# Context keys and values in float32 parts, first expert weights in idle buffers, token low parts on GpSimd: a mixture-of-experts kernel on one core

## The chip, the core and the metric

The kernel is one program on one core of a Trainium2 chip. The core has a matrix engine (PE), a vector engine (DVE), an activation engine (ACT), GpSimd (POOL), and SyncE (SP), which here does nothing but issue DMA transfers from DRAM. The metric is the time of one execution on the device in microseconds; lower is better.

## What is computed

The reference is a first block (a hybrid mixer, cross attention to a memory, a mixture of 32 experts) and a second block (a hyena branch, differential attention over the tokens and over a context, a feed-forward part), for 256 tokens of width 1024 in float32. The parts that matter here:

```python
# mixture of experts: top group, then top 2 of its 8 experts
hb = jax.nn.silu(xb @ w1[e]) * (xb @ w3[e])      # w1, w3: 1024 x 512
return hb @ w2[e]                                # w2: 512 x 1024
...
return rmsnorm(x, norm_f_g)                      # end of the first block
...
# second block: keys and values of the context, 256 rows
hc = modulate(rmsnorm_2(ctx, g_mix_pre[layer]), csh1, csc1)
kv_c = hc @ w_in[layer][:, OFF_K:OFF_G]          # 512 columns of keys, 512 of values
...
k_all = jnp.concatenate([k, k_c], axis=1)
v_all = jnp.concatenate([v, v_c], axis=1)
```

The context keys and values depend on nothing in the first block, and nothing reads them before the attention of the second block.

## The kernel before

**Weights.** Every weight goes through a ring of 1 MB buffers ("slots") in the order of the code. `wtile` takes the next slot, and the load into it, issued by SP, waits for the product that read the slot last. SP issues in order, so one load that waits holds back all loads behind it. `change_ring` adds or removes slots: during the expert stage there are 16, and from pair 6 on, when `filters` gives ten of them to other uses, 8.

**Two kinds of product.** `dense` and `dense_T` take a float32 product apart into three faster ones: `split` makes a high part of each weight block (`wh`, ACT, L303) and a low part (`wl`, DVE, L304), and PE multiplies high by high, high by low, low by high (L315 to L317, L351 to L353). The expert stage multiplies float32 directly (L1274, L1304).

**Order of the work around the change.** After the cross attention (`wxo`) the tokens are transposed and multiplied by the router's weights (`lg`). DVE then works out the routing: which token goes to which slot of which expert, as matrices `hot` (L938). In the same stretch ACT and DVE make high and low parts of the normed tokens, `xnh` (L868) and `xnl` (L869), with a stride of 8 elements. PE gathers tokens by products of `xnh` and `xnl` with `hot` (`pxg`, L944), ACT copies them to `xg` (L945), and the first expert product can start. PE's waiting times in routing are filled with the context products: `ctx_k` (keys) and `ctx_v` (values), both three-part, both ahead of the first expert product.

**The expert stage** runs over 16 pairs of experts, j = 0 to 15. For each, `up` takes w1 (`hw1`, four loads of 1 MB) and w3 (`hw3`, four loads), and `down` of the pair before takes w2 (four loads): 192 MB in all. A half of `up` is two loads and is named `kb` 0 or 1 below. Between them stand the scatter of results (`py`), the gather for the next pairs (`pxg`) and, from pair 7 on, pieces of the hyena filters (`f` to `fH`).

**After the last pair** the first block's last norm runs on ACT, DVE and POOL, and its result `xs` is transposed (L273) and split for the second block's first products.

A list scheduler orders the instructions of each engine; `issue_after` and `pe_after` place an instruction behind another one on its engine.

Of the kernel before, what the change touches and what calls it, by code (L numbers as in the profile page):

```python
# [8 lines left out]
F32 = mybir.dt.float32  # L9
# [8 lines left out]
P = 128  # L18
D = 1024
S = 256  # L20
# [81 lines left out]
def _body(nc, tc, I, out, ctx, dbg):  # L102
# [28 lines left out]
    def f(t):  # L131
        return t.bitcast(F32)
# [32 lines left out]
    def wloads(wsrc, c0, n, KB=8):  # L165
        return [wload(wsrc[kb * P:(kb + min(4, KB - kb)) * P, c0:c0 + n], min(4, KB - kb), n) for kb in range(0, KB, 4)]
# [109 lines left out]
    def tr_split(src, KB, gcol=None, sc=1.0, bcol=None, hl=None, name="t", g="A"):  # L276

        hi, lo = hl if hl else (xTt(name + "h", g), xTt(name + "l", g))
        for kk in range(0, KB, 2):
            pv = tr4(src, kk)  # L280
            if gcol is None:
                hilo(hi[:, kk:kk + 2, :], lo[:, kk:kk + 2, :], pv, sc)
                continue
            for j in range(2):
                k = kk + j
                if bcol is None:
                    hilo(hi[:, k, :], lo[:, k, :], pv[:, j, :], gcol[:, k:k + 1])
                else:
                    last["hi"] = A.activation(hi[:, k, :], pv[:, j, :], AF.Identity, bias=bcol[:, k:k + 1],  # L289
                                              scale=gcol[:, k:k + 1])  # L290
                    lo_of(lo[:, k, :], hi[:, k, :], pv[:, j, :], gcol[:, k:k + 1], bcol[:, k:k + 1])
        return hi, lo
# [43 lines left out]
    def dense_T(xh, xl, KB, ws, n, consume, ahead=None):  # L336


        nb = n // P
        accs = [acc().rearrange("p (b s) -> p b s", b=2) for _ in range(0, nb, 2)]  # L340
        for k in range(KB):
            if ahead:
                ahead(k)
            h, l = split(ws[k // 4][:, k % 4, :], n)
            if pend:
                pend.pop(0)()
            for b in range(nb):
                s = slice(b * P, (b + 1) * P)
                p = accs[b // 2][:, b % 2, :]

                T.matmul(p, h[:, s], xh[:, k, :], start=k == 0 and b % 2 == 0, stop=False)  # L351
                T.matmul(p, h[:, s], xl[:, k, :], start=False, stop=False)  # L352
                T.matmul(p, l[:, s], xh[:, k, :], start=False, stop=k == KB - 1 and b in (nb - 1, b // 2 * 2 + 1))  # L353
            if k % 4 == 3 and after:
                after.pop(0)()
        for i, p in enumerate(accs):
            consume(i, p[:, :min(2, nb - 2 * i), :])
# [42 lines left out]
    def copy_to(dst, **kw):  # L400
        def c(t, p):
            A.activation(dst[:, t, :], p, AF.Copy, **{k: v[:, t:t + 1] for k, v in kw.items()})
        return c
# [401 lines left out]
    softmax(0)  # L805
    softmax(1)
    wxo = [wloads(I["w_xo"][0], ch * 512, 512) for ch in range(2)]
    wck = [wloads(I["w_in_2"][0], 2048 + ch * 512, 512) for ch in range(2)]
    for ch in range(2, 4):
        dense(mh, ml_, 8, W["w_xkv", ch], 512, copy_to(vx[:, :, (ch - 2) * 512:(ch - 1) * 512], scale=rm))  # L810
    oh, ol = xTt("oh", "A"), xTt("ol", "A")
# [11 lines left out]
    rc = rsq(sumsq(cx), 2, 1.0 / D)  # L823
    for t in range(2):
        V.tensor_scalar(cx[:, t, :], cx[:, t, :], rc[:, t:t + 1], None, op0=OP.mult)
    ch_, cl_ = tr_split(cx, 8, mods[:, 1, :], bcol=mods[:, 6, :], name="cx", g="B")
    for ch in range(2):
        dense(oh, ol, 8, wxo[ch], 512, add_x(ch))
    tap("x2", x)
# [19 lines left out]
    xmT = xgt("xmT")  # L849
    for kk in range(0, 8, 2):  # L850
        pv = tr4(x, kk)
        A.activation(xmT[:, kk, :], pv[:, 0, :], AF.Copy, scale=g_moe[:, kk:kk + 1])
        V.tensor_scalar(xmT[:, kk + 1, :], pv[:, 1, :], g_moe[:, kk + 1:kk + 2], None, op0=OP.mult)
    rxm = rsq(sumsq(x), 2, 1.0 / D, name="rxm", pl=mo)
    p = smp("lg")
# [4 lines left out]
    def in_block(v, k):  # L860
        return v.rearrange("t (p k) -> t k p", k=k)

    def by_row(v, k):
        return v.rearrange("t (k p) -> t k p", k=k)

    xn = [xTt(nm, "A", F32R, (P, 2, D)) for nm in ("xnh", "xnl")]
    for t in range(2):
        A.activation(by_row(xn[0][:, t, :], 8), in_block(x[:, t, :], 8), AF.Copy, scale=rxm[:, t:t + 1])  # L868
        V.scalar_tensor_tensor(by_row(xn[1][:, t, :], 8), in_block(x[:, t, :], 8), rxm[:, t:t + 1],  # L869
                               by_row(f(xn[0][:, t, :]), 8), op0=OP.mult, op1=OP.subtract)  # L870
    lg = mo.tile([P, 2, 36], F32, name="lg")
    for t in range(2):
        V.scalar_tensor_tensor(lg[:, t, :], p[:, 36 * t:36 * t + 36], rxm[:, t:t + 1], brt, op0=OP.mult, op1=OP.add)
# [85 lines left out]
    V.tensor_copy(pre_, p[:, :96].rearrange("p (c n) -> p c n", c=3))  # L959


    def ctx_k():
        def c_kc(i_, p):
            A.activation(kTc[:, 2 * i_:2 * i_ + 2, :], p, AF.Copy)
        dense_T(ch_, cl_, 8, wck[0], 512, c_kc)

    def ctx_v():
        dense(ch_, cl_, 8, wck[1], 512, copy_to(vc))
        change_ring(["xTB"] * 2)
    ctx_k()  # L970
    ctx_v()


    ge = mo.tile([P, 2, 4], F32, name="ge")
# [157 lines left out]
    def filters():  # L1132
# [5 lines left out]
        wc = late["wc"] = ExitStack()  # L1138
        wpC = late["wpC"] = wc.enter_context(tc.tile_pool(name="wpC", bufs=2, side="right", reuse_waits="tile"))
        change_ring([wpC] * 2, (wpB,))  # L1140
        fctx = late["fctx"] = ExitStack()
        fp = fctx.enter_context(pool("fp", "right"))
        dft = fp.tile([P, 2, 2, S], F32, name="dft")
# [89 lines left out]
    def erows(nm, e, b0, n):  # L1233

        return I[nm][0, e].rearrange("(p k) n -> p k n", p=P)[:, b0:b0 + n, :]

    def eload(nm, e, kb, k, n):
        v = wtile(k, n)
        nc.sync.dma_start(v, erows(nm, e, kb * k, k))
        return v  # L1240

    def norm_part(t, hf, xs):

# [24 lines left out]
    def up(j, nm, hps, kbs):  # L1268
        s0 = (j % 2) * P
        for kb in kbs:  # L1270
            we = [eload(nm, 2 * j + e, kb, 4, 512) for e in range(2)]
            for k in range(4):
                for e in range(2):
                    traced[:] = [T.matmul(hps[64 * e:64 * e + 64, :], xgs[j][:, 4 * kb + k, s0 + 64 * e:s0 + 64 * e + 64], we[e][:, k, :],  # L1274
                                start=kb + k == 0, stop=kb + k == 4)]

    def act_half(hps):
# [12 lines left out]
    def down(j, hT):  # L1290
        po = [acc("po0"), acc("po1")]
        for kb in range(2):
            if j < NJ - 1:
                we = [eload("w2", 2 * j + e, kb, 2, 1024) for e in range(2)]
            else:

                we = [wtile(2, 1024) for e in range(2)]
                for q in range(2):
                    for e in range(2):
                        nc.sync.dma_start(we[e][:, q, :], erows("w2", 2 * j + e, 2 * kb + q, 1)[:, 0, :])  # L1300
            for q in range(2):
                for hf in range(2):
                    for e in range(2):
                        traced[:] = [T.matmul(po[hf][64 * e:64 * e + 64, :], hT[:, 2 * kb + q, 64 * e:64 * e + 64],  # L1304
                                    we[e][:, q, hf * 512:(hf + 1) * 512], start=kb + q == 0, stop=kb + q == 2)]
        return po

    def gather_some(n):
# [19 lines left out]
    for j in range(NJ):  # L1328
        if j == 2:
            with pe_after():  # L1330
                po = down(1, hT)
            with pe_after():
                gather_some(2)
            after_down(1, po)
            hT = None
            traced.clear()
            overflow(n_over)
            traced.clear()
        if j % 2 == 0 and j + 2 < NJ:
            xg_, st_ = group(j + 2)  # L1340
            xgs[j + 2] = xgs[j + 3] = xg_
            todo += st_
        h1 = acc("hw1")
        with pe_after():
            up(j, "w1", h1, (0, 1))
        sg = act_half(h1)
        if j in (6, 15):
            hooks[j]()
        po = None
        if hT is not None:  # L1350
            with pe_after():
                po = down(j - 1, hT)
        h3 = acc("hw3")
        with pe_after():
            up(j, "w3", h3, (0, 1))
        V.tensor_tensor(by_row(sg, 4), by_row(sg, 4), in_block(h3, 4), op=OP.mult)  # L1356
        if j == 0:
            lambdas()
            n_over = nc.values_load(novi[0:1, 0:1], min_val=0, max_val=7)
            with pe_after():  # L1360
                bc_rows(rows[:, 0], dest)
                bc_rows(rows[:, 1], gt)
        if po is not None:
            after_down(j - 1, po)
        with pe_after():
            gather_some(4)
        if 6 < j < 15 and j in hooks:
            with pe_after():
                hooks[j]()
        with pe_after():  # L1370
            hT = turn(sg)
    with pe_after():
        po = down(NJ - 1, hT)
    after_down(NJ - 1, po, norm_part)
    tap("x3", x)
    moctx.close()

# [18 lines left out]
    with tc.issue_after(last["hi"].ins):  # L1396
        for t in range(2):
            A.activation(x[:, t, :], xr[:, t, :], AF.Copy, scale=r1[:, t:t + 1])
    tap("xp", x)
    late["wc"].close()  # L1400
    set_ring([wpA] * NA)
# [294 lines left out]
```

## Time and profile before

| | |
|---|---|
| median of 3 runs | 1289.45 us (1285.69 to 1291.61) |
| the profiled execution: its own time, its span | 1290.93 us, 1289.1 us |
| PE, DVE, ACT, POOL busy in the span | 1234.1, 747.4, 552.7, 69.3 us |
| bytes moved | 365.29 MB, mean 283 GB/s |

The span goes from the first to the last instruction of the profiled execution. A busy time counts how long an engine had an instruction, not what that instruction could have taken at best. Positions ("at 388.22") are microseconds from the start of the span.

### The profile page before, as it was taken

To read this page: it belongs to the slowest core of one execution; us is meant where nothing else is said; L and a number is where in the kernel's file an instruction comes from. 1 tells how busy PE (TensorE), PEld (TensorE's weight loads), DVE (VectorE), ACT (ScalarE), POOL (GpSimd) and SP (SyncE) were. 2 spreads that over 40 slices of the span, in tenths; PEclk is the share of its full clock that TensorE was granted. 3 is DMA by queue.
4 is the path that set the end of the run, shared out by engine and by line. 5 is a ranking of instruction groups with operands and counts; after the bars stand their busy time and mean duration, and the time that the engine had idled before them with its cause. 6 is when DMAs were issued, how large, how long until landed. Compare 5 with 4: busy or idle time off the path is not lost.

```text
span 1289.1 us, 18195 instructions
## 1 busy us (share of the span) xinstructions
PE 1234.1 (96%) x6920; PEld 891.3 (69%) x6920; DVE 747.4 (58%) x1474; ACT 552.7 (43%) x1016; POOL 69.3 (5%) x118
## 2 busy tenths in 40 slices
PE   7999999999999999999999999969999998899996
PEld 7887788897884444433334444449877996799985
DVE  6996888747671413213241341259898788667654
ACT  6867455756561112111111211146256556455552
POOL 1101100100000000100000000010000101000000
PEclk9999999999999999999999999979999999999998
DMA  9764774994439999999999999976453576566751
GB/s 348 260 212 153 272 236 157 389 383 153 165 110 403 419 420 420 400 420 421 421 407 407 421 420 404 419 288 235 158 180 131 204 187 229 187 227 196 234 188 49
DMA packets 103243, 365.29 MB, mean 283 GB/s; under 512 B 6840, under 2 KB 9203, under 8 KB 78960
## 3 DMA queue, kind: packets, MB, share of 16 engines
q1 hardware_dynamic: 93264, 329.77, 68.0%
q0 software_dynamic: 9744, 34.18, 7.8%
q8 instruction: 56, 0.92, 0.3%
q14 instruction: 35, 0.29, 0.1%
q10 hardware_dynamic: 144, 0.14, 0.1%
HBM read 363.00 MB, written 1.06 MB: 282 GB/s over the span
## 4 chain that ended last, share of the span: by engine, by line
PE 51%; DMA 8%; issue 3%; DVE 2%; ACT 1%; POOL 1%; SPq 0%; DVEq 0%; POOLq 0%; ACTq 0%
PE hw L1274 13%; DMA w<-in_w_dram 6%; PE acc L352 5%; PE acc L351 5%; PE acc L353 5%; PE po L1304 4%; PE acc L317 2%; PE acc L315 2%; PE acc L316 2%; PE py L1022 2%; PE pxg L944 2%; PE iy L1463 1%; PE fH L1213 1%; PE s L1505 1%; DMA w<-in_w_ffn_gate_dram 1%
## 5 line engine op out<-in xcount | busy, mean ns | idle before, releaser
L303 ACT ACTIVATE wh<-w 128x512 fp32r<-128x512 f32 (+1 forms) x454 | 279.0, 622 | 234.4 <-PE acc L352 91.3
L304 DVE TENSOR_TENSOR wl<-w,wh 128x512 fp32r<-128x512 f32 (+1 forms) x454 | 302.7, 682 | 128.4 <-ACT wh L303 125.8
L1274 PE MATMUL hw<-w,xg 128*64 128x512 f32 x1024 | 236.3, 595 | 14.5 <-DMA w<-in_w_dram 12.6
L1274 PEld LDWEIGHTS hw<-w,xg 128*64 128x64 f32 x1024 | 79.8, 137 | 155.2 <-issue 127.5
L245 DVE SCALAR_TENSOR_TENSOR otl<-po,gs,oth 128x512 fp32r<-128x512 f32 x32 | 23.9, 748 | 209.0 <-ACT oth L244 208.2
L1304 PE MATMUL po<-w,hT 128*64 128x512 f32 x512 | 120.1, 595 | 2.6 <-ACT hT L1287 1.5
L1304 PEld LDWEIGHTS po<-w,hT 128*64 128x64 f32 x512 | 45.2, 137 | 71.4 <-issue 61.4
L945 ACT ACTIVATE xg<-pxg,vec 128x256 f32<-128x256 f32 x64 | 29.3, 475 | 139.0 <-PE pxg L944 138.3
L352 PE MATMUL acc<-xfl,wh 128*128 128x256 f32 x288 | 80.7, 280 | 0.0
L351 PE MATMUL acc<-xfh,wh 128*128 128x256 f32 x288 | 80.4, 279 | 0.0
L353 PE MATMUL acc<-xfh,wl 128*128 128x256 f32 x288 | 80.3, 279 | 0.0
L458 DVE SCALAR_TENSOR_TENSOR junk<-waT,cb 128x1024 bf16<-128x1024 f32 x64 | 77.9, 1217 | 4.2 <-DMA waT<-in_l_waT_dram 3.8
L316 PE MATMUL acc<-wl,xmh 128*128 128x512 f32 x192 | 76.8, 400 | 1.2 <-DVE wl L304 1.2
L317 PE MATMUL acc<-wh,xml 128*128 128x512 f32 x192 | 76.6, 399 | 0.0
L315 PE MATMUL acc<-wh,xmh 128*128 128x512 f32 x192 | 75.8, 399 | 0.0
L1356 DVE TENSOR_TENSOR sg<-sg,hw 128x512 f32<-128x512 f32 x16 | 11.0, 688 | 107.5 <-PE hw L1274 107.5
L244 ACT ACTIVATE oth<-po,gs 128x512 fp32r<-128x512 f32 x32 | 22.0, 687 | 101.3 <-PE po L1304 101.2
L352 PE MATMUL acc<-x2l,wh 128*128 128x256 f32 x224 | 63.1, 284 | 0.5 <-DVE x2l L251 0.5
L351 PE MATMUL acc<-x2h,wh 128*128 128x256 f32 x224 | 63.1, 287 | 0.3 <-ACT x2h L289 0.3
L353 PE MATMUL acc<-x2h,wl 128*128 128x256 f32 x224 | 63.3, 284 | 0.0
L351 PEld LDWEIGHTS acc<-xfh,wh 128*128 128x128 f32 x288 | 54.1, 188 | 0.0
L352 PEld LDWEIGHTS acc<-xfl,wh 128*128 128x128 f32 x288 | 54.1, 188 | 0.0
(542 smaller groups left out, 2557.7 us busy)
## 6 DMA issues: line engine op xcount, KB each, us to landing
w<-in_w_dram SPq DMA_DIRECT2D x188, 1024.0 KB, 13.7
w<-in_w_in_dram SPq DMA_DIRECT2D x54, 1024.0 KB, 6.7
waT<-in_l_waT_dram POOLq DMA_DIRECT2D x48, 512.0 KB, 5.5
w<-in_w_ffn_gate_dram SPq DMA_DIRECT2D x10, 1024.0 KB, 5.2
w<-in_w_ffn_up_dram SPq DMA_DIRECT2D x10, 1024.0 KB, 5.2
w<-in_w_ffn_down_dram SPq DMA_DIRECT2D x10, 1024.0 KB, 5.3
w<-in_w_out_dram SPq DMA_DIRECT2D x8, 1024.0 KB, 5.6
w<-in_w_xkv_dram SPq DMA_DIRECT2D x8, 1024.0 KB, 14.2
```

Source lines behind the costliest of these rows:

```text
L303: last["act"] = A.activation(h[:, :n], w, AF.Copy)
L304: last["dve"] = V.tensor_tensor(l[:, :n], w, f(h[:, :n]), op=OP.subtract)
L315: T.matmul(p, xh[:, k, s], h[:, :n], start=k == 0, stop=False)
L316: T.matmul(p, xh[:, k, s], l[:, :n], start=False, stop=False)
L317: T.matmul(p, xl[:, k, s], h[:, :n], start=False, stop=k == KB - 1)
L351: T.matmul(p, h[:, s], xh[:, k, :], start=k == 0 and b % 2 == 0, stop=False)
L352: T.matmul(p, h[:, s], xl[:, k, :], start=False, stop=False)
L353: T.matmul(p, l[:, s], xh[:, k, :], start=False, stop=k == KB - 1 and b in (nb - 1, b // 2 * 2 + 1))
L458: V.scalar_tensor_tensor(junk(), w[i_][:, b, :], 1.0, cb[:, r_, :], op0=OP.mult, op1=OP.mult, accum_out=adac[:, n, r_:r_ + 1])
L945: A.activation(xg[:, k, :], p, AF.Copy, scale=col["l_gmoe"][:, k:k + 1])
L1274: traced[:] = [T.matmul(hps[64 * e:64 * e + 64, :], xgs[j][:, 4 * kb + k, s0 + 64 * e:s0 + 64 * e + 64], we[e][:, k, :], start=kb + k == 0 ...
L1304: traced[:] = [T.matmul(po[hf][64 * e:64 * e + 64, :], hT[:, 2 * kb + q, 64 * e:64 * e + 64], we[e][:, q, hf * 512:(hf + 1) * 512], start= ...
```

## The change

The three-part products of the context with all their splits are gone. The context, normed and transposed, stays in float32 (`cxT`), and its keys and values are direct float32 products in four parts. Half the keys stand in the routing. The other half is issued from j = 0, behind w3. The first half of the values comes at j = 4, with its own load in the expert queue. The second half stands behind the last `py`, with its load behind the last w2, and is added to the first by DVE. Ahead of the expert stage 2 MB of value weights are not loaded any more, and three of the first four w1 loads go into buffers outside the ring: one of the two `xg` buffers, the four `wh` tiles and the four `wl` tiles. Token low parts are made by POOL in eight operations instead of two on DVE, with a scratch tile `xt` from the `wl` tiles.

```diff
-    wck = [wloads(I["w_in_2"][0], 2048 + ch * 512, 512) for ch in range(2)]
+    wck = wloads(I["w_in_2"][0], 2048, 512)
...
-    ch_, cl_ = tr_split(cx, 8, mods[:, 1, :], bcol=mods[:, 6, :], name="cx", g="B")
+    cxT = xTt("cxT", "B", F32)
...
+            A.activation(cxT[:, k, :], pv[:, j, :], AF.Identity, bias=mods[:, 6, k:k + 1], scale=mods[:, 1, k:k + 1])
+    change_ring(["xTB"])
...
-    for t in range(2):
-        A.activation(by_row(xn[0][:, t, :], 8), in_block(x[:, t, :], 8), AF.Copy, scale=rxm[:, t:t + 1])
-        V.scalar_tensor_tensor(by_row(xn[1][:, t, :], 8), in_block(x[:, t, :], 8), rxm[:, t:t + 1],
-                               by_row(f(xn[0][:, t, :]), 8), op0=OP.mult, op1=OP.subtract)
+    with tc.issue_after(xm_act.ins):
+        for t in range(2):
+            A.activation(by_row(xn[0][:, t, :], 8), in_block(x[:, t, :], 8), AF.Copy, scale=rxm[:, t:t + 1])
+            for hf in range(2):
+                s = slice(hf * 512, (hf + 1) * 512)
+                xt = wk.tile([P, 512], F32, name="xt", tag="wl", bufs=4)
+                G.tensor_scalar(by_row(xt, 4), in_block(x[:, t, :], 8)[:, 4 * hf:4 * hf + 4, :], rxm[:, t:t + 1], None,
+                                op0=OP.mult)
+                G.tensor_tensor(xn[1][:, t, s], xt, f(xn[0][:, t, s]), op=OP.subtract)
...
-    def ctx_k():
...
-    ctx_k()
-    ctx_v()
+    kc = [acc("kc") for _ in range(2)]
+
+    def ctx_k(hf):
+        for k in range(4 * hf, 4 * hf + 4):
+            for b in range(4):
+                traced[:] = [T.matmul(kc[b // 2][:, b % 2 * S:(b % 2 + 1) * S], wck[hf][:, k % 4, b * P:(b + 1) * P],
+                                      cxT[:, k, :], start=k == 0 and b % 2 == 0, stop=k == 7 and b % 2 == 1)]
...
+    def ctx_v(wv, cT):
+        pv = [acc("cv") for _ in range(2)]
+        for k in range(4):
+            for t in range(2):
+                traced[:] = [T.matmul(pv[t], cT[:, k, t * P:(t + 1) * P], wv[:, k, :], start=k == 0, stop=k == 3)]
+        return pv
+    ctx_k(0)
...
+        A.activation(cxh, cxT[:, 4:8, :], AF.Copy)
+        change_ring(["xTB"])
...
+    def first_load(e, kb):
+
+        src = erows("w1", e, kb * 4, 4)
+        if (e, kb) == (0, 0):
+            v = mo.tile([P, 4, 512], F32, name="w0", tag="xg", bufs=2)
+        elif (e, kb) == (1, 1):
+            return eload("w1", e, kb, 4, 512)
+        else:
+            ts = [wk.tile([P, 512], F32, name="w0", tag="wh" if e else "wl", bufs=4) for k in range(4)]
+            for k in range(4):
+                nc.sync.dma_start(ts[k], src[:, k, :])
+            return ts
+        nc.sync.dma_start(v, src)
+        return [v[:, k, :] for k in range(4)]
...
         if j == 0:
             lambdas()
+            with pe_after():
+                ctx_k(1)
...
+        if j == 4:
+            wv = ctx_v_load(0)
+            with pe_after():
+                for t, p in enumerate(ctx_v(wv, cxT[:, 0:4, :])):
+                    A.activation(vc[:, t, :], p, AF.Copy)
...
+    wv = ctx_v_load(1)
     after_down(NJ - 1, po, norm_part)
+
+    with pe_after():
+        pcv = ctx_v(wv, late["cxh"])
...
+    for t in range(2):
+        V.tensor_tensor(vc[:, t, :], pcv[t], vc[:, t, :], op=OP.add)
```

The order that the scheduler makes of it, at three places. First PE at the end of routing and in pair 0, before; `acc` is the last block of the context values, `hw_4108` is the w1 product of pair 0 and `hw_4135` its w3 product:

```order
L316 MATMUL acc<-wl,cxh 128x512
L317 MATMUL acc<-wh,cxl 128x512
L1274 MATMUL hw_4108<-w,xg 64x512 x16
L1274 MATMUL hw_4135<-w,xg 64x512 x16
L1129 MATMUL lam<-ls,ca 128x1
L999 MATMUL prow<-ca,dest 128x128 x4
```

The same place now, where `kc` are the context keys and `w_3892` is the load in the `xg` buffer:

```order
L955 MATMUL pxg<-hot,xnl 128x256
L1151 MATMUL lam<-ls,ca 128x1
L978 MATMUL kc<-cxT,w 128x256 x6
L1314 MATMUL hw_3891<-w_3892,xg 64x512
L1314 MATMUL hw_3891<-w_3894,xg 64x512
L1314 MATMUL hw_3891<-w_3892,xg 64x512
```

The values have gone from the place ahead of the first expert product. Six key products stand there instead, and that product now reads `w_3892`.

Second SP in the stretch of the first expert loads, now. `w0_3894` to `w0_3897` go to the `wh` tiles, `w0_3910` to `w0_3913` to the `wl` tiles, `w0_3892` to the `xg` buffer, the others to the ring (`w_4080` and `w_4082` are w2 of pair 0, `w_4093` and `w_4105` are w3 of pair 1):

```order
L1279 DMA w_4080<-in_w2_dram 128x2048
L1272 DMA w0_3894<-in_w1_dram 128x512
...
L1272 DMA w0_3910<-in_w1_dram 128x512
L1272 DMA w0_3911<-in_w1_dram 128x512
L1272 DMA w0_3912<-in_w1_dram 128x512
L1272 DMA w0_3913<-in_w1_dram 128x512
L1279 DMA w_4082<-in_w2_dram 128x2048
L1274 DMA w0_3892<-in_w1_dram 128x2048
L1402 TENSOR_LOAD novi_3878
...
L1279 DMA w_4093<-in_w3_dram 128x2048
L1279 DMA w_4105<-in_w3_dram 128x2048
```

Before, the expert loads stood in the order in which they are used, w1 of pair 0 first. Now the w1 loads outside the ring stand behind thirteen others, and `w0_3892`, which the first expert product needs, is the last of all.

Third PE after the last pair, now (`cxh` is the copy of the second half of `cxT`):

```order
L1044 MATMUL py<-oth,ET 128x512
L1044 MATMUL py<-otl,ET 128x512 x2
L991 MATMUL cv<-w,cxh 128x512 x8
L273 MATMUL tp<-ca,xs_6797 128x128 x8
L351 MATMUL acc<-x2h,wh 128x256 x2
```

Before, the transposes `tp` of `xs` followed `py` directly.

## Rows read from the trace of the kernel before

**Rows 1.** The page, its first line.

```profile
span 1289.1 us, 18195 instructions
```

**Rows 2.** Busy time by window: PE, PEld, DVE, ACT, POOL, PE clock, DMA share, GB/s.

```profile
360.00:380.00 20.00, 18.95 (x138) 17.34 (x138) 17.75 (x62) 11.43 (x19) 0.59 (x1) 1.00 0.33 111
...
400.00:520.00 120.00, 117.19 (x586) 52.83 (x582) 33.32 (x78) 20.60 (x38) 0.00 (x0) 1.00 1.01 420
...
745.00:851.00 106.00, 104.55 (x478) 47.47 (x474) 28.99 (x56) 16.31 (x29) 0.54 (x1) 1.00 1.01 412
```

**Rows 3.** What PE waited for, 388 to 541, then 541 to 745.

```profile
PE hw L1274 <- DVEq L1037: 1.9, 1, 1.9
PE po L1304 <- ACT hT L1287: 0.7, 1, 0.7
...
PE hw L1274 <- DMA w<-in_w_dram: 12.6, 10, 1.6
```

**Rows 4.** Timelines of DVE, ACT and PE: last `hot`, last `xg`, first expert product.

```profile
378.03 0.48 DVE L938 SCALAR_TENSOR_TENSOR hot<-cm__3683,dg,hit 128x256 fp32r<-128x256 f32 x1
...
382.05 0.46 ACT L945 ACTIVATE xg<-pxg,vec 128x256 f32<-128x256 f32 x1
...
388.22 1.08 PE L1274 MATMUL hw<-w,xg 128*64 128x512 f32 x4
```

**Rows 5.** Groups of PE and DVE from 353 to 389, by line.

```profile
L315 PE MATMUL acc<-wh,cxh 128*128 128x512 f32 x16 | 6.4, 400 | 0.0
...
L304 DVE TENSOR_TENSOR wl<-w,wh 128x512 fp32r<-128x512 f32 x14 | 9.6, 683 | 0.8 <-ACT wh L303 0.7
L869 DVE SCALAR_TENSOR_TENSOR xnl<-x,rxm,xnh 128x1024 fp32r<-128x1024 f32 x2 | 4.6, 2326 | 1.8 <-ACT xnh L868 1.8
```

**Rows 6.** Timelines of POOL and ACT at 357 to 363, and POOL's large operation.

```profile
357.54 0.72 POOL L230 TENSOR_TENSOR rxm<-rxm,nhalf 128x2 f32<-128x2 f32 x1
...
358.29 4.47 ACT L868 ACTIVATE xnh<-x,rxm 128x1024 fp32r<-128x1024 f32 x2
...
L563 POOL TENSOR_TENSOR wsT<-wsT,cbm 128x1024 f32<-128x1024 f32 x1 | 3.5, 3547 | 13.5 <-DMA wsT<-in_l_wsT_dram 13.5
```

**Rows 7.** The page, DMA issues: one transfer at a time, median to landing.

```profile
w<-in_w_ffn_gate_dram SPq DMA_DIRECT2D x10, 1024.0 KB, 5.2
```

**Rows 8.** PE timeline, direct float32 products of 128x512.

```profile
691.07 1.88 PE L1213 MATMUL fH<-hsm,dft 128*128 128x512 f32 x4
692.78 1.05 PE L1217 MATMUL fH<-ca,vec 128*128 128x128 f32 x8
```

**Rows 9.** Two expert loads at pair 6: place of issue, then time to landing.

```profile
L1239 SPq DMA_DIRECT2D w<-in_w_dram x1: 384/384/384, 526.1 to 526.1; - x1
...
DMA to landing us min/median/max: 20.4/20.4/20.4
...
L1239 SPq DMA_DIRECT2D w<-in_w_dram x1: 327/327/327, 540.8 to 540.8; - x1
...
DMA to landing us min/median/max: 8.1/8.1/8.1
```

**Rows 10.** After the last pair: PE timeline, windows, DVE timeline.

```profile
852.46 0.63 PE L1022 MATMUL py<-otl,ET 128*128 128x512 f32 x2
860.73 1.56 PE L273 MATMUL tp<-ca,xs 128*128 128x128 f32 x6 [7.64 <-DVE xs L1393]
...
855.00:861.00 6.00, 0.27 (x2) 0.22 (x2) 4.95 (x14) 5.04 (x12) 1.89 (x3) 0.54 0.13 49
861.00:869.00 8.00, 7.18 (x32) 6.48 (x32) 6.62 (x14) 6.49 (x12) 2.30 (x4) 0.50 0.76 259
...
880.00:900.00 20.00, 20.00 (x177) 20.00 (x177) 19.86 (x40) 13.51 (x25) 2.12 (x4) 1.00 0.76 254
...
860.19 0.88 DVE L1393 TENSOR_SCALAR xs<-xr,r 128x512 f32<-128x512 f32 x2 [0.61 <-POOL r L1388]
...
863.86 0.42 DVE L251 TENSOR_TENSOR x2l<-tb,x2h 128x256 fp32r<-128x256 f32 x1
```

More of the change, by code (lines that the diff above doesn't have):

```diff
@@ L825, in _body @@
         V.tensor_scalar(cx[:, t, :], cx[:, t, :], rc[:, t:t + 1], None, op0=OP.mult)
-    ch_, cl_ = tr_split(cx, 8, mods[:, 1, :], bcol=mods[:, 6, :], name="cx", g="B")
+    cxT = xTt("cxT", "B", F32)
+    for kk in range(0, 8, 2):
+        pv = tr4(cx, kk)
+        for j in range(2):
+            k = kk + j
+            A.activation(cxT[:, k, :], pv[:, j, :], AF.Identity, bias=mods[:, 6, k:k + 1], scale=mods[:, 1, k:k + 1])
+    change_ring(["xTB"])
     for ch in range(2):
@@ L959, in _body, with ctx_v_load @@
     V.tensor_copy(pre_, p[:, :96].rearrange("p (c n) -> p c n", c=3))
-    def ctx_k():
[L963 to L969, printed above, removed]
-    ctx_k()
-    ctx_v()
+    kc = [acc("kc") for _ in range(2)]
[4 more added lines that the diff above has]
+                                      cxT[:, k, :], start=k == 0 and b % 2 == 0, stop=k == 7 and b % 2 == 1)]
+        if hf:
+            for i_ in range(2):
+                A.activation(kTc[:, 2 * i_:2 * i_ + 2, :], kc[i_].rearrange("p (b s) -> p b s", b=2), AF.Copy)
+    def ctx_v_load(hf):
+        return wload(I["w_in_2"][0][4 * hf * P:4 * (hf + 1) * P, 2560:3072], 4, 512)
+    def ctx_v(wv, cT):
[5 more added lines that the diff above has]
+    ctx_k(0)
     ge = mo.tile([P, 2, 4], F32, name="ge")
@@ L1140, in filters @@
         change_ring([wpC] * 2, (wpB,))
+        cxh = late["cxh"] = wc.enter_context(pool("cxp", "right")).tile([P, 4, S], F32, name="cxh")
+        A.activation(cxh, cxT[:, 4:8, :], AF.Copy)
+        change_ring(["xTB"])
         fctx = late["fctx"] = ExitStack()
@@ L1239, in eload @@
         nc.sync.dma_start(v, erows(nm, e, kb * k, k))
-        return v
+        return [v[:, i_, :] for i_ in range(k)]
     def norm_part(t, hf, xs):
@@ L1270, in up @@
         for kb in kbs:
-            we = [eload(nm, 2 * j + e, kb, 4, 512) for e in range(2)]
+            we = [first_load(e, kb) if (j, nm) == (0, "w1") else eload(nm, 2 * j + e, kb, 4, 512) for e in range(2)]
             for k in range(4):
                 for e in range(2):
-                    traced[:] = [T.matmul(hps[64 * e:64 * e + 64, :], xgs[j][:, 4 * kb + k, s0 + 64 * e:s0 + 64 * e + 64], we[e][:, k, :],
+                    traced[:] = [T.matmul(hps[64 * e:64 * e + 64, :], xgs[j][:, 4 * kb + k, s0 + 64 * e:s0 + 64 * e + 64], we[e][k],
                                 start=kb + k == 0, stop=kb + k == 4)]
@@ L1300, in down @@
                         nc.sync.dma_start(we[e][:, q, :], erows("w2", 2 * j + e, 2 * kb + q, 1)[:, 0, :])
+                we = [[v[:, q, :] for q in range(2)] for v in we]
             for q in range(2):
@@ L1304, in down @@
                         traced[:] = [T.matmul(po[hf][64 * e:64 * e + 64, :], hT[:, 2 * kb + q, 64 * e:64 * e + 64],
[L1305 removed]
+                                    we[e][q][:, hf * 512:(hf + 1) * 512], start=kb + q == 0, stop=kb + q == 2)]
         return po
```

2 lines of the change are left out of this document (1 added, 1 removed).

## Prediction

> **What bounds the kernel now.** I read the windows first, then PE's waits, then the timelines around the places that the change touches. In the expert stage the windows [rows 2] show the DMA share at 1.01 and 420 GB/s from 400 on: the transfers never pause. But PE is as full there, 117.19 of 120 us, and 104.55 of 106 at the stage's end. Which of the two is late last is read from the waits [rows 3]: from 388 to 541 PE waits 2.6 us and for no transfer at all, from 541 to 745 it waits 12.6 us for weights. So the stage has two limits in turn: PE until pair 6, then the DMA stream; at the end PE has little room again. In routing it is otherwise: from 360 to 380 the DMA share is 0.33 [rows 2], since the ring is full, and the first expert product is at 388.22 [rows 4]. The last gathered tokens are there at 382.05 + 0.46 = 382.5 [rows 4]; the 5.7 us between are the end of `ctx_v`. [...]
>
> **The start of the stage.** Removed are `ctx_v`'s end (5.7 us) and, on DVE, `xnl` (4.6 us) and 14 weight splits (9.6 us) [rows 5], which stand between the routing's small operations; the last `hot` is at 378.03 [rows 4]. I take 9 of these 14.2 us as lying in the routing's path, so the gather would end at 382.5 − 9 = 373.5. Six key products follow. Their price comes from direct float32 products of 128x512: four records, which are two products, take 692.78 − 691.07 = 1.71 us [rows 8], 0.86 each; the keys have half the columns, 0.43 each as an estimate. Six take 2.6: PE is ready at 376.1.
>
> It must also have its weights, and these now hang on POOL. `w0_3892` stands on SP behind the four loads into the `wl` tiles, and each of those waits for a POOL subtraction that frees its scratch tile. POOL begins when `rxm` is ready, 357.54 + 0.72 = 358.3, and its first subtraction needs half of `xnh`, 358.29 + 2.24 = 360.5 [rows 6]. No POOL operation of 128x512 is in the trace. The nearest is 3547 ns for 1024 elements [rows 6], 1.77 us for 512, which is an upper bound for the subtraction; the lower is DVE's 0.68 [rows 5]. For the strided multiplication the lower bound is DVE's contiguous 0.44 [rows 10]; the upper one is DVE's strided 2326/2 = 1163 ns [rows 5] times POOL's handicap, 1.77/0.68 = 2.6, so 3.0 us. I take 1.6 and 1.25, near POOL's own row, as its multiplication has one large input instead of two. Then POOL ends at 360.5 + 1.6 + 3 × 2.85 = 370.7. The bounds give 364.7 and 377.4.
>
> From there to `w0_3892`: one load alone takes 5.2 us [rows 7]; 0.25 MB for the last `wl` tile and 1 MB of w2 go ahead of it at 420 GB/s [rows 2], 3.1 us; one more issue on SP takes 0.4 [rows 9]. Sum 8.7: it lands at 379.4. So the first expert product moves from 388.22 to 379.4, **8.8 us earlier**, with bounds of 376.1 (PE's readiness) and 386.1 (slow POOL).
>
> [...]
>
> **What is added in the stage.** Ten key products in pair 0 (10 × 0.43 = 4.3 us) and eight value products at j = 4 (8 × 0.86 = 6.9): 11.2 us on PE, all before pair 6, where PE is the late one and has no wait to put them in [rows 3]. The waits that are there, for a branch and for `hT`, stay. So in pair 6 PE is 11.2 − 8.8 = 2.4 us later than now, although it began 8.8 earlier. Before, these products ran in three parts at 0.4 us a record of 512 [rows 5], overlapping, ahead of the stage.
>
> Whether that matters is decided at the ring's shrinking. Now, with 16 slots, the first two w2 loads of pair 5 are issued by 526.1, and only the third, at 540.8, waits for the first half of `hw1` of pair 6. The second lands at 526.1 + 20.4 = 546.5; the third takes 8.1 us [rows 9], 2.9 more than a lone load, so the queue has 2.9 us of work left when it joins. After the change there is one `xTB` slot less until `cxT` is copied in `filters`, 15 in place of 16, so already the second load waits for that half of `hw1`. It is issued at 540.8 + 2.4 = 543.2, into a queue that has by then nothing left, and lands 5.2 later at 548.4: **1.9 us later** than before. From here the transfers are the limit, each of 2.5 us behind the other, and PE's 12.6 us of waits take up its own lateness. At the stage's end I expect +1.9 us. With the first product at its bounds it is (376.1: PE 0.9 earlier than now) −1.4, or (386.1) +8.6.
>
> Elsewhere the parts are hidden: the copies to `vc` and `cxh` run on ACT, which is busy 20 of 120 us [rows 2]; the extra 1 MB for the first values costs 2.5 us of a stream that the slots hold up anyway at pair 6; the last one goes behind the last w2 and ahead of weights that wait for the norm.
>
> **After the last pair.** The second eight value products, 6.9 us, start when `py` ends, 852.46 + 0.63 = 853.1, and end at 860.0, ahead of the transposes at 860.73 [rows 10]: they fit by 0.7 us. They fill the gap behind which PE ran at half clock. From 861 to 869 PE is busy 7.18 us at 0.50 [rows 10]; at full clock that would be 3.6 us less. Two additions of 128x512 on DVE, 0.68 each [rows 5], cost 1.4 us, since they stand ahead of the first `x2l` (863.86), for which PE waits. And from 880 to 900 DVE is busy 19.86 of 20 us [rows 10], so a faster PE meets a full DVE. Bounds: −3.6 if all the clock's gain arrives, +1.4 if none; I take the middle, −1.1.
>
> [...]
>
> **Sum.** +1.9 − 1.1 = +0.8 us on the profiled execution's 1290.93, the span of 1289.1 [rows 1] and 1.8 around it. That execution is 1.5 us above the median of 1289.45, so I forecast 1290.2 for the median: no change that can be told from none (about 0.5%, 6.4 us, is what a measurement of this kernel tells).
>
> **Rivals.** (a) *The early start is kept.* If the transfers do not run dry at pair 6, because PE gets there sooner or slots come free earlier, the stream alone sets the end: 8.8 earlier less 2.5 for the extra load is −6.3, less what the queue idles early in the stage for want of free slots, down to about −3. With the tail's −1.1 to −3.6 this gives −4 to −10: 1279.5 to 1285.5, around 1283. For it: 12.6 us of PE's waits show that PE has room later. Against it: none of that room lies before 541. Faster than 0.5% in two thirds of this case. (b) *POOL is slow.* All hangs on one load behind eight POOL operations. At the upper bounds the first product is at 386.1, the stage ends 8.6 late, with the tail +7.5: 1297. It decides for slower when the product comes after 385.0, so POOL ends after 376.3: operations of 2.3 us on average instead of 1.45. For it: the stride of 8, and no row of POOL with one. Against: its only large row. (c) *The start stays, the tail wins:* the clock is kept and DVE hides the additions, +1.9 − 3.6 = −1.7: 1287.8, within the same bound.
>
> **How the numbers follow.** Forecast 0.45, (c) 0.17, (a) 0.23, (b) 0.15. Same: 0.45 + 0.17 + a third of (a) less a little of the forecast's edges, 0.66; faster 0.18; slower 0.16. The range of 8 in 10 runs from inside (a) to inside (b): 1282.5 to 1296; the forecast's own is 1286 to 1294.
>
> **What would show it.** Right: first expert product at 377 to 382, directly behind the landing of `w0_3892`; PE without waits for weights until pair 6; there a pause of the DMA share, and the second w2 load of pair 5 landing near 548; the last product of the stage 1 to 3 us later than now; PE clock 1.00 at 860. Wrong: a first product after 384 with POOL still at work on `xt` (b), or a queue at pair 6 that never empties (a), or PE's ten and eight products in less than 11 us.

## The result and the profile after

The changed kernel takes 1301.59 us (median of 7 runs, 1300.53 to 1302.74), the kernel before 1290.83 in the same comparison (7 runs, 1285.69 to 1297.13): a ratio of 1.01 with a 95% interval of [1.0083, 1.0116]. It is slower by 1%, and outside the range of 1282.5 to 1296. The profiled execution took 1301.31 us.

The page's first line and its engines, beside [rows 1]:

```profile
span 1299.6 us, 18069 instructions
PE 1241.7 (96%) x6872; PEld 890.1 (68%) x6872; DVE 733.4 (56%) x1442; ACT 543.2 (42%) x1001; POOL 82.0 (6%) x126
```

The span is 10.5 us longer, and PE is busy 7.6 us longer. Where, the windows tell, in the columns of [rows 2] (two answers):

```profile
362.00:366.00 4.00, 2.46 (x12) 1.82 (x10) 4.00 (x22) 0.21 (x1) 4.00 (x3) 1.00 0.00 0
366.00:370.00 4.00, 0.86 (x4) 0.86 (x5) 3.96 (x5) 0.20 (x1) 4.00 (x4) 0.87 0.39 128
370.00:374.00 4.00, 3.35 (x11) 2.44 (x11) 3.15 (x18) 0.00 (x0) 0.23 (x1) 0.50 0.44 134
374.00:378.00 4.00, 3.93 (x18) 3.96 (x19) 0.97 (x3) 1.42 (x4) 0.60 (x1) 0.50 0.92 313
378.00:382.00 4.00, 2.82 (x19) 2.61 (x18) 1.43 (x6) 2.32 (x6) 0.00 (x0) 0.85 0.51 213
443.00:449.00 6.00, 0.00 (x0) 0.00 (x0) 2.03 (x4) 0.00 (x0) 0.00 (x0) 0.87 1.01 414
449.00:452.00 3.00, 2.65 (x8) 0.93 (x10) 2.65 (x8) 0.00 (x0) 0.00 (x0) 0.50 1.01 421
452.00:456.00 4.00, 4.00 (x16) 1.36 (x14) 1.00 (x6) 0.00 (x0) 0.00 (x0) 0.72 0.23 90
```

```profile
400.00:520.00 120.00, 112.74 (x548) 52.12 (x547) 32.56 (x76) 20.60 (x38) 0.00 (x0) 0.97 0.96 393
```

From 366 to 370 DVE is busy 3.96 of 4 us with five instructions, where 22 fitted into the 4 us ahead, and PE does nearly nothing; its clock then falls to 0.50. From 443 to 449 PE does nothing at all, and its clock falls again. Before, the clock was 1.00 over 360 to 380 and over 400 to 520 [rows 2]. The other places are read from timelines of PE (start, duration, what ran):

```profile
381.54 0.38 PE L1151 MATMUL lam<-ls,ca 1*128 1x1 f32 x2 [1.18 <-DVE ls L1149]
381.85 2.86 PE L978 MATMUL kc<-cxT,w 128*128 128x256 f32 x12
384.63 13.95 PE L1314 MATMUL hw<-w,xg 128*64 128x512 f32 x64
...
398.52 4.58 PE L978 MATMUL kc<-cxT,w 128*128 128x256 f32 x20
...
518.25 7.03 PE L991 MATMUL cv<-w,cxT 128*128 128x512 f32 x16
...
551.07 2.37 PE L1314 MATMUL hw<-w,xg 128*64 128x512 f32 x10
...
862.57 0.73 PE L1044 MATMUL py<-oth,ET 128*128 128x512 f32 x2
...
864.88 7.03 PE L991 MATMUL cv<-w,cxh 128*128 128x512 f32 x16
872.69 1.22 PE L273 MATMUL tp<-ca,xs 128*128 128x128 f32 x8 [0.79 <-DVE xs L1445]
```

The first expert product is at 384.63, 3.6 us earlier than at 388.22 [rows 4], not 8.8. Pair 6's w1 products start at 551.07, against 537.15 before: 13.9 later, not 2.4. The last product of the stage ends at 862.56, against 850.63: 11.9 later, not 1.9. The transposes of `xs` keep that distance, 872.69 against 860.73 [rows 10], and the end of the span, 10.5 later, regains 1.4 us of it.

What PE waited for, in three stretches (353 to 385, 384 to 555, 555 to 750), beside [rows 3]:

```profile
PE pp L923 <- DVE ea L921: 4.7, 1, 4.7
PE lam L1151 <- DVE ls L1149: 1.2, 1, 1.2
```

```profile
PE hw L1314 <- PEq L1059: 6.4, 1, 6.4
PE po L1345 <- ACT hT L1327: 0.7, 1, 0.7
```

```profile
PE hw L1314 <- DMA w<-in_w_dram: 11.7, 9, 1.3
PE po L1345 <- DMA w<-in_w_dram: 1.1, 2, 0.6
```

Two waits are new: 4.7 us for DVE's `ea`, in routing, and 6.4 us for PE's own sequencer at L1059, behind pair 1. There the program jumps over a block that handles an overflow. Each engine has that jump; this is PE's row of it, min, median and max in ns, now and (L1037) before:

```profile
L1059 PEldq COMPARE_BRANCH  x1: 6205/6205/6205, 442.8 to 442.8; - x1
```

```profile
L1037 PEldq COMPARE_BRANCH  x1: 445/445/445, 442.4 to 442.4; - x1
```

The same branch at the same time takes 5.8 us more (ACT's and DVE's rows of it are 45 and 72 ns in both kernels). During it, from 446 to 447, a queue that the trace names `instruction` carries one piece of 16 KB (16384 bytes; over the span it carries 0.90 MB in 55 pieces). Before, such a piece came from 434 to 436, ahead of the branch. Piece, megabytes and share of the DMA engines, now and before:

```profile
q8 instruction: 1, 0.02, 6.9%
```

```profile
q8 instruction: 1, 0.02, 3.4%
```

In routing, DVE's timeline beside POOL's shows the other one. First POOL, then DVE's instructions of 1.0 us or more and one ordinary one of the same kind:

```profile
357.08 8.20 POOL L879 TENSOR_SCALAR xt<-x,rxm 128x512 f32<-128x512 f32 x4
365.24 4.99 POOL L881 TENSOR_TENSOR xnl<-xt,xnh 128x512 fp32r<-128x512 f32 x4
```

```profile
361.30 1.15 DVE L893 TENSOR_TENSOR E<-lg,f1m 128x64 f32<-128x64 f32 x1
...
363.05 0.21 DVE L896 TENSOR_TENSOR E<-E,f1w 128x64 f32<-128x64 f32 x1
...
363.33 1.15 DVE L913 SCALAR_TENSOR_TENSOR el<-E,lg 128x64 f32<-128x64 f32 x1
...
365.55 1.04 DVE L896 TENSOR_TENSOR E<-E,f2w 128x64 f32<-128x64 f32 x1
366.52 1.23 DVE L1008 TENSOR_TENSOR ee<-m 128x2 f32<-128x2 f32 x1
...
367.92 1.17 DVE L921 TENSOR_TENSOR ea<-E 128x64 f32<-128x64 f32 x1
369.01 1.24 DVE L1011 TENSOR_SCALAR den<-ee 128x2 f32<-128x2 f32 x1
```

The same `E` operation takes 0.21 us in one place and 1.04 in another. POOL's four multiplications end near 359.1, 361.2, 363.2 and 365.2, its subtractions at 366.5, 367.7, 369.0 and 370.2 (equal parts of the two rows). After 360.77, where the routing begins, six POOL operations start, and six DVE instructions are long: one for each. Those beside a subtraction end when it ends (at 366.6, 367.8, 369.1 and 370.3); beside a multiplication DVE's next ones are short again (0.15 us, at 362.38 and 364.41) while POOL still works. Four take 0.8 to 0.95 more than such an operation does alone, `ee` and `den` 1.08 (the rows for alone stand below, where POOL's part is given back): in sum near 5.8 us.

### The profile page after: what moved, and what is told of

Read it like the earlier page. It is cut to its first block, busy times and chain, and to the rows that moved or that the text cites. A ratio compares the mean times of both kernels' runs of the same rounds, so it can differ in the third digit from the quotient of the medians.

```text
span 1299.6 us, 18069 instructions
## 1 busy us (share of the span) xinstructions
PE 1241.7 (96%) x6872; PEld 890.1 (68%) x6872; DVE 733.4 (56%) x1442; ACT 543.2 (42%) x1001; POOL 82.0 (6%) x126
## 4 chain that ended last, share of the span: by engine, by line
PE 53%; DMA 8%; DVE 2%; ACT 1%; issue 1%; POOL 0%; SPq 0%; DVEq 0%; POOLq 0%; ACTq 0%
PE hw L1314 14%; DMA w<-in_w_dram 6%; PE acc L352 5%; PE acc L351 5%; PE acc L353 5%; PE po L1345 4%; PE acc L317 2%; PE acc L316 2%; PE acc L315 2%; PE py L1044 2%; PE pxg L955 2%; PE iy L1517 1%; PE fH L1238 1%; PE s L1559 1%; DMA w<-in_w_ffn_gate_dram 1%
## 5 line engine op out<-in xcount | busy, mean ns | idle before, releaser
L303 ACT ACTIVATE wh<-w 128x512 fp32r<-128x512 f32 (+1 forms) x438 | 268.8, 622 | 237.6 <-PE acc L317 92.6
L304 DVE TENSOR_TENSOR wl<-w,wh 128x512 fp32r<-128x512 f32 (+1 forms) x438 | 290.8, 679 | 131.5 <-ACT wh L303 129.9
## 6 DMA issues: line engine op xcount, KB each, us to landing
w<-in_w_xkv_dram SPq DMA_DIRECT2D x8, 1024.0 KB, 14.2
```

The costliest lines, as they stand in the source:

```text
L303: last["act"] = A.activation(h[:, :n], w, AF.Copy)
L304: last["dve"] = V.tensor_tensor(l[:, :n], w, f(h[:, :n]), op=OP.subtract)
```

## The experiments

Each changes the branch, POOL's part, both, or the place of the added products. "First product" is the start of the first expert product, "stage end" the end of the last product of the stage (before 388.22 and 850.63, after 384.63 and 862.56). Ratios are to the kernel before on the same chip.

**The branch, cured in the changed kernel.** 36 products of 8x8 at the program's start move PE's code and do nothing else.

```diff
+    pd = tpp("pd")
+    for _ in range(36):
+        T.matmul(pd[0:8, 0:8], nhalf, nhalf, start=True, stop=True)
```

> The changed kernel with 36 more PE products of 8x8 ahead of everything else (their result is not read), so that all later PE instructions stand further on in the program; nothing else is moved. Theory A (the changed kernel's 6.2 us in PE's branch at the end of pair 1 is the fetch of PE's code, which now comes too late because of where the code is cut into 16 KB pieces): the branch falls below 1 us, the half clock behind it goes too, and the time falls by about 6.9 us to 1293 to 1296. Rival (the branch is slow because the transfers are busy or because of what stands around it): the branch stays at 5 to 7 us and the time within 2 us of 1301.6.

Measured: 1295.27 us, ratio 1.0062 [1.0043, 1.0082], 6.3 us less than the changed kernel. The jump takes 445 ns, pair 6 starts at 545.2 and the stage ends at 858.19. The waits of PE from 384 to 552 are back to those of [rows 3]:

```profile
PE hw L1317 <- DVEq L1062: 1.8, 1, 1.8
PE po L1348 <- ACT hT L1330: 0.7, 1, 0.7
```

**The branch, brought into the kernel before**, with 30 such products.

> The kernel before with 30 more PE products of 8x8 ahead of everything else, which should put the pieces of PE's code about where they lie in the changed kernel. Theory A: the branch at the end of pair 1 takes 4 to 7 us instead of 0.44, and the time rises by 4 to 7 us to 1294 to 1298. Rival: the branch stays at 0.4 us, time 1289 to 1291.

The stall came, as this row shows (the jump takes 6165 ns), and pair 6 is 6.4 us later, at 543.6:

```profile
PE hw L1277 <- PEq L1040: 6.3, 1, 6.3
```

But the stage ends only 3.1 us later (853.69). Of the 3.4 us made up behind pair 6, PE's recorded waits show 1.1 (14.4 us instead of 15.5); where the rest was is not shown. The time is 1291.16, ratio 1.0017 [0.9997, 1.0037]: no difference that can be told. In the profiled execution the last 3 us are regained in the feed-forward part, where the clock falls at different places in different executions (from 1110 to 1115 it is 0.66 in the kernel before and 1.00 here; in the changed kernel it is 0.93 from 1085 to 1110). So it is shown in both directions that the code's position sets the length of the jump; that it costs time also in the kernel before is not.

The traces of all thirteen kernels agree on what goes with it. The pieces of that queue are some 250 PE instructions apart (247 from 474.82 to 499.82 in the changed kernel). In the nine traces with a short jump, one piece comes 5.5 to 7.1 us ahead of the jump and the next 3.7 to 3.9 us behind its start. In the four with a long jump none comes in the 20 us ahead; the first comes 3.6 to 3.7 us behind its start, and the jump ends some 2.5 us after that.

**POOL's part given back to DVE** in the changed kernel.

```diff
-            for hf in range(2):
...
-                G.tensor_scalar(by_row(xt, 4), ...)
-                G.tensor_tensor(xn[1][:, t, s], xt, f(xn[0][:, t, s]), op=OP.subtract)
+            V.scalar_tensor_tensor(by_row(xn[1][:, t, :], 8), in_block(x[:, t, :], 8), rxm[:, t:t + 1],
+                                   by_row(f(xn[0][:, t, :]), 8), op0=OP.mult, op1=OP.subtract)
```

> The changed kernel with the token low parts on DVE again (two operations of 1024 elements), everything else as changed. Theory A (POOL's operations hold up DVE: six of DVE's small routing operations take 1.0 to 1.2 us instead of 0.15 to 0.22): no DVE operation of the routing takes over 0.5 us, the last matrix of the first gather is ready some 2.5 us sooner although DVE has 4.6 us more to do, and the first expert product comes at 381 to 383 instead of 384.6; time 1298 to 1301. Rival (the slow operations come from something else, and POOL took load off DVE): they stay slow, the first product comes 3 to 5 us later than 384.6, time 1304 to 1307.

Measured: 1296.2 us, ratio 1.0057 [1.0039, 1.0074], 5.4 us less, which is more than was expected. No routing operation is long; three that were:

```profile
366.92 0.15 DVE L1004 TENSOR_TENSOR ee<-m 128x2 f32<-128x2 f32 x1
...
367.30 0.23 DVE L917 TENSOR_TENSOR ea<-E 128x64 f32<-128x64 f32 x1
367.44 0.16 DVE L1007 TENSOR_SCALAR den<-ee 128x2 f32<-128x2 f32 x1
```

DVE pays 4.13 us for the low parts, and still the first product is 3.7 us earlier, at 380.90. The stage ends at 859.65, 2.9 earlier; the other 2.5 us lie behind it and have no cause shown. The two operations that were to leave DVE [rows 5] cost less on it than POOL's help does.

**POOL working beside it, for nobody.** The kernel just shown, plus the same eight POOL operations into a tile that nothing else uses.

```diff
+            for hf in range(2):
+                s = slice(hf * 512, (hf + 1) * 512)
+                xt = wk.tile([P, 512], F32, name="xt", tag="junk", bufs=1)
+                G.tensor_scalar(by_row(xt, 4), in_block(x[:, t, :], 8)[:, 4 * hf:4 * hf + 4, :], rxm[:, t:t + 1], None,
+                                op0=OP.mult)
+                G.tensor_tensor(xt, xt, f(xn[0][:, t, s]), op=OP.subtract)
```

> The changed kernel with the token low parts on DVE, and besides the same eight POOL operations on the same data, whose results nobody reads and whose scratch is a tile that nothing else uses: no instruction waits for POOL. Theory A (POOL's operations hold up DVE's small ones by their mere presence): four to six of DVE's routing operations take 1.0 to 1.3 us instead of 0.15 to 0.23, the first expert product is 3 to 6 us later than the 380.9 of the version without POOL work, time 1299 to 1303. Rival B (the stretched rows are waits for something that POOL's results bring): no stretched operation, first expert product at 381, time 1296.

Measured: 1303.23 us, ratio 1.0111 [1.0086, 1.0136], 7.0 more than without. Its POOL and its long DVE rows:

```profile
359.65 3.05 POOL L883 TENSOR_TENSOR xt<-xt,xnh 128x512 f32<-128x512 f32 x1 [0.15 <-ACT xnh L875]
362.80 3.59 POOL L881 TENSOR_SCALAR xt<-x,rxm 128x512 f32<-128x512 f32 x1
366.47 1.31 POOL L883 TENSOR_TENSOR xt<-xt,xnh 128x512 f32<-128x512 f32 x1
367.88 2.16 POOL L881 TENSOR_SCALAR xt<-x,rxm 128x512 f32<-128x512 f32 x1
370.12 1.27 POOL L883 TENSOR_TENSOR xt<-xt,xnh 128x512 f32<-128x512 f32 x1
371.49 2.09 POOL L881 TENSOR_SCALAR xt<-x,rxm 128x512 f32<-128x512 f32 x1
```

```profile
359.54 4.96 DVE L876 SCALAR_TENSOR_TENSOR xnl<-x,rxm,xnh 128x1024 fp32r<-128x1024 f32 x2 [1.82 <-ACT xnh L875]
366.58 1.23 DVE L1007 TENSOR_TENSOR f1m<-f1m,goh 128x8 f32<-128x8 f32 x1
368.24 1.00 DVE L896 TENSOR_TENSOR E<-E,rt__3651 128x64 f32<-128x64 f32 x1
370.19 1.23 DVE L1013 TENSOR_SCALAR den<-ee 128x2 f32<-128x2 f32 x1
371.65 1.06 DVE L1015 TENSOR_TENSOR gt<-pg,den 128x2 f32<-128x2 f32 x1
```

The last four POOL operations each have their one long DVE instruction, though none waits for POOL. And the hold goes both ways: beside DVE's two large `xnl`, POOL's second and third operations take 3.05 and 3.59 us instead of 1.3 and 2.1. The first product is 3.8 later, at 384.72, and the stage ends 3.9 later; the other 3 us of the time lie behind the stage and have no cause shown.

**Both cured.**

> The changed kernel with two things taken back and nothing else: the token low parts are made by DVE in two operations as before, and 36 dummy products of 8x8 at the program's start shift PE's code so that the branch behind pair 1 finds its target. Theory A (the two failed steps of the prediction are additive: the branch costs 6.9 us in PE's time, POOL's work beside the routing about 5): the start of the first expert product at 380 to 382, the branch 0.45, hw1 of pair 6 at 541 to 543, the last product of the stage ends at 853 to 856, time 1290 to 1293, within 0.3% of the kernel before. Rival B (both are covered by the same waits for weights, so that the second cure gives little): last product at 857 to 859, time 1294 to 1296, as with one cure alone.

Measured: 1291.94 us (12 runs), ratio 1.0023 [1.0009, 1.0037]; first product 381.62, pair 6 at 541.6, stage end 853.73, span 1290.8. The two cures add up: of the 1.0% lost, 0.2% is left, and its interval leaves out 1. What is left of the change behaves as the prediction had it: PE's waits from 555 to 750 are for weights (all but 0.4 us), and the second w2 load of pair 5 is issued at 545.23 and lands 5.1 later, at 550.4, where 543.2 and 548.4 stood for a start at 379.4. The start is 2.2 later and the load 2.0.

**POOL's part alone, in the kernel before**, first with its scratch in the `wl` tiles, then in a tile of its own.

```diff
-        V.scalar_tensor_tensor(by_row(xn[1][:, t, :], 8), in_block(x[:, t, :], 8), rxm[:, t:t + 1],
-                               by_row(f(xn[0][:, t, :]), 8), op0=OP.mult, op1=OP.subtract)
+        for hf in range(2):
+            s = slice(hf * 512, (hf + 1) * 512)
+            xt = wk.tile([P, 512], F32, name="xt", tag="wl", bufs=4)
...
```

> The kernel before with only the token low parts moved to POOL (eight operations). Theory A: DVE operations that run beside POOL stretch to over 1 us; the routing gains nothing although DVE is rid of 4.6 us; the first expert product within 388 to 391, time 1289 to 1293. Rival (POOL relieves DVE without a price): first product at 384 to 386, time 1286 to 1288.

> The kernel before with only the token low parts on POOL, as in e3, but with a scratch tile that the weight splits do not use, so that POOL and DVE share no buffer. Theory A (POOL's operations hold up DVE operations that fall beside them): several DVE operations at 357 to 372 stretched by about 1 us, so that of the 4.6 us that DVE gives up most is lost again; first expert product at 386 to 390, time 1287 to 1292. Rival (only the shared tile did the harm in e3): no stretched operation, first product at 383 to 385, time 1284 to 1287.

Measured: 1299.8 us, ratio 1.0093 [1.0069, 1.0117], first product 398.66; and 1296.72, 1.0073 [1.0048, 1.0098], first product 395.46. Both times and both starts are later than either theory said. In the first the scratch shares the `wl` tiles with the weight splits that still stand there, and those wait for POOL:

```profile
DVE wl L304 <- POOL xnl L874: 5.1, 2, 3.8
```

In the second that wait is gone and PE waits for `ea`, as in the changed kernel (POOL stretches splits there too, 1.66 us instead of 0.68):

```profile
PE pp L916 <- DVE ea L914: 5.2, 1, 5.2
```

So POOL's part alone loses time; how its 7.2 us at the start divide between held instructions, late splits and the clock stays open.

**Where the added products stand.** The branch cured, and the first value products at j = 8 instead of 4, from a copy of `cxT` that ACT puts into two `wh` tiles at pair 6:

```diff
-        if j == 4:
+        if j == 8:
...
-                for t, p in enumerate(ctx_v(wv, cxT[:, 0:4, :])):
+                for t, p in enumerate(ctx_v(wv, late["cxq"])):
```

> The kernel of e1 (changed kernel, code moved on) with the first half of the context values at pair 8 instead of pair 4; its input is copied into two idle weight-split tiles at pair 6, so that the ring changes where it did. Theory A (PE is the late one up to pair 6 and the ring then turns its lateness into lateness of the transfers, while from pair 6 to 13 PE waits for weights and 7 us more cost nothing): hw1 of pair 6 starts 6 to 7 us sooner than in e1, the last product of the stage ends 4 to 7 us sooner, time 1288 to 1291. Rival (the 7 us of PE work cost the same wherever they stand, or nothing since the transfers set the end): the last product within 2 us of e1's 858.2, time 1294 to 1297.

Measured: 1292.28 us, ratio 1.0029 [1.0013, 1.0046], 1.3 us above the range expected. Pair 6 starts at 538.5, 6.7 earlier than at j = 4, and the stage ends 4.5 earlier (853.66). Behind pair 6 PE has waits to put the seven us of products in (12.6 us of them are left there, against 15.5 with the products at j = 4); ahead of it there are none but the 2.5 us shown above.

**All of them, and a fourth** (branch, low parts on DVE, values at j = 8, and `lam` with all second-half keys behind w3 of pair 0):

```diff
         if j == 0:
-            lambdas()
             with pe_after():
+                lambdas()
                 ctx_k(1)
```

> The changed kernel with four things undone or moved at once: token low parts on DVE again, 36 small PE products ahead of everything (code position), first half of the context values at pair 8, and lambda's product and the last key products behind w3 of pair 0 instead of ahead of w1. Theory A (the four losses are these and add up): first expert product at 377 to 380, PE's branch below 1 us, hw1 of pair 6 at 533 to 537, last product of the stage 846 to 849, time 1283 to 1287. Rival (the ring and the transfers set the stage's end in any case): last product at 850 or later, time 1289 to 1292.

Measured: 1287.44 us, ratio 0.9994 [0.998, 1.0007]; first product 376.80, pair 6 at 532.7, stage end 848.65, 2.0 before that of the kernel before. The trace stands where it was expected, or 0.2 to 0.3 us ahead of it; the time is 0.4 us above the range and not different from before.

Two tries to get more from it. The second values at pair 10, so that the gap behind the last pair is empty again:

```diff
+        if j == 10:
+            wv = ctx_v_load(1)
+            with pe_after():
+                for t, p in enumerate(ctx_v(wv, [late["cxh"][:, k, :] for k in range(4)])):
+                    V.tensor_tensor(vc[:, t, :], p, vc[:, t, :], op=OP.add)
```

> The kernel of e6 with the second half of the context values at pair 10 (added there by DVE) instead of in the gap of the last norm, which is empty again as in the kernel before. Theory A (filling the gap keeps PE's clock up and gains about 1 us in the first products behind it, after what the additions cost): PE clock 0.50 behind the gap, the products behind it 0.5 to 2 us later relative to the last py, time 0 to 2 us over e6. Rival (the clock's whole half is regained): 3 us or more over e6. Second rival (the gap's products only push the norm's followers back): 1 us or more below e6.

Measured: 1295.96 us, ratio 1.0061 [1.0042, 1.0079]; the stage ends 7.8 later, 0.9 of it from the start, so the seven us of products at pair 10 reach its end, although PE still waits 8.2 us for weights from 545 on. Behind the gap the two kernels stay some 0.5 us apart, so filling it is worth about that. And half the keys at pair 3, added to the first half by DVE:

```diff
-                ctx_k(1)
...
+        if j == 3:
+            with pe_after():
+                ctx_k(1)
```

> The kernel of e6 with the second half of the context keys (16 products of 0.43 us) at pair 3 instead of behind w3 of pair 0; the first half is copied out and the second added by DVE; 52 instead of 36 small products at the start, so that PE's code ahead of the branch is as long as in e6. Theory A (in e6 the transfers pause twice, by 2.6 and 3.4 us, at 405 and 411, since PE is with the keys and frees no slots): these two pauses are gone, hw1 of pair 1 starts at 394 to 397, the last product of the stage comes at 843 to 847, time 1281 to 1285. Rival (PE's own work and not the transfers set the end of e6's stage from pair 8 on): the pauses go, but the last product stays at 847 to 850 and the time within 2 us of e6's 1287.4.

Measured: 1289.1 us, ratio 1.0005 [0.9991, 1.0019]. The transfers' pause early in the stage gets weaker and does not go: with the keys in pair 0 they moved 16 to 115 GB/s from 402 to 408, now 152 from 400 to 402 and some 210 from 406 to 410. From 539 to 545 they now run at 273 to 336 GB/s, PE then waits 1.5 us for weights up to 546.7, and the stage ends at 852.0, 3.4 later than without and beyond both theories: no gain.

## Why the prediction was wrong

**The start: the step "I take 9 of these 14.2 us as lying in the routing's path" failed, by what it left out.** It took work off DVE and put POOL beside it at no cost to DVE. But POOL's six operations beside the routing held six DVE instructions, near 5.8 us in sum, so `hot` ends at 374.83. Without them it would have ended near 369, which is where the forecast had it (378.51 − 9 = 369.5): the 9 us were about right, the price of POOL was missing. The kernel with POOL working for nobody shows that presence is enough. POOL's own end came out as forecast, 370.2 against 370.7, but by luck: its multiplications took 2.08 us instead of 1.25, its subtractions 1.28 instead of 1.6, it began 1.2 us sooner, and all four multiplications ran ahead of the subtractions.

PE stood idle while DVE was held, and its clock was at 0.50 from 369 to 379: the gather's 256-column products follow each other at 0.21 us where they do so at 0.11 near 380, at full clock. That some 23 of 32 ran so costs some 2.3 us; the clock falls there without POOL's part as well (with the low parts on DVE it is 0.50 from 370 to 374 and 0.65 from 374 to 378). `lam`, now ahead of the six key products, waits 1.2 more. So PE was ready at 384.6 and not at 376.1, and it came last: the load `w0_3892`, on which all was made to hang, was there at 380.8 (379.4 forecast), before its product. The start gained 3.6 instead of 8.8: 5.2 us short. Giving POOL's part back to DVE returns 3.7 of them, after the 4.13 us that DVE pays; how the rest divides between clock and `lam` no run separates. All the long instructions but `den` read two tensors or two parts of one; `den` (1.24 us instead of 0.16) has one input of two columns. What the two engines contend for no run shows.

**In the stage: a term was missing.** "The waits that are there, for a branch and for `hT`, stay" was the failed step. The branch went from 0.45 to 6.2 us, and PE, idle for 6 us, ran at half clock (0.50) from 449 to 454. With the branch cured pair 6 comes 6.9 us sooner behind the first product. Shifting PE's code by 36 products removes it (445 ns), and shifting the unchanged kernel by 30 makes it (6165 ns), so it depends on where PE's code lies. That the time goes into fetching the target's code was not shown: it fits the pieces of all thirteen traces, but no run changed the fetching itself.

**What held.** The products: eight value products 7.03 us (6.9 forecast), ten key products 4.58 (4.3), together 10.6 more from the first product to pair 6 with the branch cured (11.2). The mechanism at pair 6 held too: PE later, no free slot, a queue that runs empty. With both faults PE was 13.9 late there instead of 2.4, and the transfers paused for most of the 6 us up to the load of 554.75:

```profile
549.00:555.00 6.00, 5.99 (x37) 3.03 (x37) 5.28 (x14) 3.18 (x6) 0.00 (x0) 1.00 0.06 20
```

From there 11.7 us of waits for weights were left, about as before, so nearly all the lateness reached the end.

The tail came out at −1.4 against −1.1, which is close in part by luck. Only 0.7 us are gained behind the gap (the same product comes 173.0 us behind the stage's end instead of 173.7); the rest arises in the feed-forward, where executions differ by more than that: from the stage's end to the span's end the changed kernel takes 437.1 us, and with the branch cured, with the same operations there, 433.5. PE's clock is 1.00 until 877 and 0.72 from there to 883: it was kept over the gap and lost behind it, where PE waits 0.79, 0.60 and 1.26 us for `xs`, `x2h` and `x2l`.

So the sum is: forecast +0.8, the start +5.2, the branch +6.9, less 2.1 (the products were 0.6 cheaper, and 1.5 more than forecast was made up behind pair 6) and 0.3 in the tail: +10.5, which is the span's. Rival (b) gave the nearest time, 1297, but its condition did not come: POOL ended at 370.2, not after 376.3. With both cured the forecast of no change was 0.2% off.

## What to carry to other kernels

Moving elementwise work from a full DVE to an idle POOL was not free for DVE here: each POOL operation of 1.3 or 2.1 us held one DVE instruction for about 1 us, so beside a chain of small DVE operations count POOL's instructions and add that. An edit that adds or removes instructions also moves the code of every later branch: here 36 small products took PE's jump from 6.2 us to 0.45, and 30 took it from 0.45 to 6.2. Compare the branch rows of both traces before looking for the cause in the edit itself. A product that is "free" because it fills a wait is free only on the side of the program where the engine waits: at pair 10 the 7 us reached the end, and moving 7 us from j = 4 to j = 8 brought the end forward by 4.5.

## What was unexpected of the hardware

A DVE operation on 128x2 elements took 1.23 us beside a POOL subtraction, and POOL's multiplication 3.59 us instead of 2.1 beside DVE's large one. POOL's strided multiplication of 128x512 (2.08 us, one large input) is slower than its contiguous subtraction with two (1.28). A jump over unused code cost PE 6.2 us or 0.45 by the code's position alone, with the weight stream at a DMA share of 1.01 beside it. And in an otherwise equal part of the program, the feed-forward, spans differ by some 3 us between executions, with the granted clock falling at different places (437.1 us from the stage's end in the changed kernel, where it is 0.93 from 1085 to 1110; 433.5 with the branch cured, where it is 1.00 there and 0.99 from 1115 to 1230): that is as much as the gains that were looked for at the end.
